# Four inner norms of a two-layer decoder trunk: roots by 32x32 turns on VectorE and a power on GpSimd instead of matmuls and an iteration

## The chip, the cores and the metric

The kernel runs on one core of one Trainium2 chip. The metric is device time in microseconds (us) of one execution; the value shown for a kernel is the median of its runs. A core has five engines that run beside each other, each in its own fixed order: TensorE (PE in the profile, with its weight loads as PEld), VectorE (DVE), ScalarE (ACT), GpSimd (POOL) and SyncE (SP, which here issues most DMAs). They wait for each other through semaphores. Matmuls accumulate in PSUM banks; everything else lies in SBUF.

## The reference, cut to what matters

The input is one sequence of 256 tokens of width 1024, in float32. There are two layers. Every norm is an RMS norm: each token is divided by the root of the mean of its squares (plus a small constant), and multiplied by a gain.

```python
def rms_norm(x, g):
    xf = x.astype(jnp.float32)
    y = xf * lax.rsqrt(jnp.mean(xf * xf, axis=-1, keepdims=True) + EPS)
    return (y * g.astype(jnp.float32)).astype(x.dtype)

# layer 0
x = x + short_conv_mixer(rms_norm(x, a_norm), a_w_in, a_conv, a_w_out)
x = x + conv_glu_ffn(rms_norm(x, f_norm[0]), f_w_up[0], f_conv[0], f_conv_b[0], f_w_down[0])
# layer 1
k_blk, v_blk, k_mean = shared_kv(x, kv_norm, w_k, w_v)
x = x + moba_attention(rms_norm(x, b_norm), w_q, w_o, k_blk, v_blk, k_mean, rel_bias)
x = x + conv_glu_ffn(rms_norm(x, f_norm[1]), f_w_up[1], f_conv[1], f_conv_b[1], f_w_down[1])
return rms_norm(x, final_norm)
```

`conv_glu_ffn` is an up projection to 2 x 2816, a causal convolution of width 3 along the tokens, silu(g) * v, and a down projection. The K/V norm and the norm of the attention see the same x, so they share one root per token and differ in their gains. That leaves four inner roots: mixer, feed-forward 0, shared K/V with queries, feed-forward 1. The final norm is computed in another way and is not touched.

## The kernel before

**Layout.** Activations stand transposed: `xT` is 128 partitions by 8 tiles by 256 tokens, so a token's features are spread over the partitions. Every float32 operand of a matmul is split into a high and a low part, and a product is three matmuls (`mm3`, lines 169 to 171: high x high, high x low part of x, low part of the weights x high).

**Weights.** They come in units: big ones ("B", 1 MB, in three raw buffers) and small ones ("S", 0.5 MB). For each unit a DMA fills `rawB` or `rawS`, ScalarE writes the high part (`hiB`, `hiS`, line 91) and VectorE the low part (`loB`, `loS`, line 97), which reads raw and high part. `hi("B")` and `lo("B")` take the next unit in order; `lo` then issues the DMA of the unit three later. The high and low buffers have two or three slots: `hi` of a unit waits until TensorE has finished the earlier unit in that slot. In the attention's part there are two slots, and the units come in the order v0, v1, v2, q0 to q7, v3 (v: values, q: queries and keys of two heads).

**Order.** Every engine's order is the order in which the program's lines issue instructions; there is no scheduler behind it. TensorE runs the units one after another without a break in the program: `up_step` for mixer and feed-forward, `v_step` and `qk_step` for the attention, 48 matmuls for each big unit.

**The roots.** The division by the root is put off: the matmuls take x times gain, and the roots are multiplied into the product as it leaves PSUM (`mixer_a` lines 456 and 465, `conv` line 551, `qk_out` line 678), or by columns for the values (`v_out`, lines 662 and 663). So the roots are wanted only when the first product is done. At each boundary `boundary()` adds the residual, writes the high and low parts of x (lines 283 and 287) and the squares (291), and adds the squares' tiles up to one row of 128 x 256 (296 to 299). Two helpers then make the roots:

- `rstd_cols` sums the 128 partitions by a matmul with a column of ones (line 342; its result stands as columns, token on partition), scales (346), takes the inverse root by a guess and three iterations on VectorE (327 to 332), and writes a diagonal matrix in a high and a low part (353, 354).
- `rstd_rows` multiplies a matrix of ones (`each`) with that diagonal (361), which gives every partition the whole row of roots, and ScalarE copies it to `rr` (364).

Some steps of TensorE's work are put between these two, so that the iteration has time; tile 0 of x is copied to a second address (`tile_0_again`, lines 278 and 279) for units that take tile 0 late. `bias_table` (lines 370 to 382) makes a table of the attention's bias on GpSimd at the program's start; it is stored to DRAM at line 630 and read in the attention.

In the attention's part `v_step(1)` carries the sums, `v_step(2)` the spreading; ScalarE's queue there holds the split of v2, then of q0, then `v_out(0)`, then the copy of the roots.

Of the kernel before, what the change touches and what calls it, by code (L numbers as in the profile page):

```python
# [13 lines left out]
I32 = mybir.dt.int32  # L14
# [28 lines left out]
def yoco_kernel(ctx: ExitStack, tc: tile.TileContext, t: dict, out: bass.AP):  # L43
# [95 lines left out]
    each = const.tile([128, 192], F32R, name="each")[:, 48:176]  # L139
# [5 lines left out]
    A.activation(each, ones, AF.Copy)  # L145
# [158 lines left out]
    def boundary(acc, x, gain, order=same, again=True):  # L304
# [20 lines left out]
    def rsqrt(ms, y, a, eng=V):  # L325

        eng.tensor_scalar(y.bitcast(I32), ms.bitcast(I32), -0.5, float(0x5F3759DF), op0=OP.mult, op1=OP.add)
        for _ in range(3):
            eng.tensor_mul(a, y, y)
            if eng is V:  # L330
                V.scalar_tensor_tensor(a, a, -0.5, ms, op0=OP.mult, op1=OP.mult)
                V.scalar_tensor_tensor(y, a, 1.5, y, op0=OP.add, op1=OP.mult)
            else:
                eng.tensor_mul(a, a, ms)
                eng.tensor_scalar(a, a, -0.5, 1.5, op0=OP.mult, op1=OP.add)
                eng.tensor_mul(y, a, y)

    def rstd_cols(sq, meanwhile=None):

        ps = psum.tile([128, 512], F32, name="misc", bufs=1)  # L340
        for c in range(2):
            PE.matmul(ps[:, c:c + 1], sq[:, 2, c * 128:(c + 1) * 128], ones[:, 0:1],
                      start=(c == 0), stop=True, skip_group_check=True)
        w = tmp.tile([128, 8], F32, name="nw")
        ms, y, a = w[:, 0:2], w[:, 2:4], w[:, 4:6]
        V.tensor_scalar(ms, ps[:, 0:2], 1.0 / D, EPS, op0=OP.mult, op1=OP.add)
        rsqrt(ms, y, a)
        if meanwhile:
            meanwhile()
        dh, dl = (tmp.tile([128, 384 + 64], F32R, name="d" + x, tag="z" + x, bufs=4)[:, 16:16 + S] for x in "hl")  # L350
        for c in range(2):
            d = slice(c * 128, c * 128 + 128)
            V.tensor_scalar(dh[:, d], ident, y[:, c:c + 1], None, op0=OP.mult)
            V.scalar_tensor_tensor(dl[:, d], ident, y[:, c:c + 1], f32(dh[:, d]), op0=OP.mult, op1=OP.subtract)
# [131 lines left out]
    for q in range(1, 4):  # L486
        quarter(q)
# [556 lines left out]
```

## Time and profile before

| | |
|---|---|
| Median of 3 runs | 568.18 us (567.7 to 568.34) |
| Profiled execution, its own time | 567.42 us |
| Its span, first to last instruction | 565.6 us |
| Mean granted TensorE clock | 0.997 |
| TensorE busy | 558.5 us, 99% of the span, 4908 matmul records |
| VectorE busy | 473.2 us, 84% |
| ScalarE busy | 341.7 us, 60% |
| GpSimd busy | 10.3 us, 2% |

How to read the rows quoted below: a row of the timeline has its start and its duration in us, the engine, the line in the kernel, the operation, output<-inputs with shapes, and xN where N like operations are merged (then the duration is from the first start to the last end). What stands in square brackets is idle time ahead of it, and what ended it. A row of a group has the count, then busy us, then the mean ns of one, then the idle time before. A float32 matmul that is not split by hand shows as several records (line 342: x4 for two). In the row of one tile's instructions, three numbers parted by strokes are the shortest, median and longest duration in ns.

### The profile page before, as it was taken

What the parts mean: (1) busy time and instruction counts of PE and PEld (TensorE: products, weight loads), DVE (VectorE), ACT (ScalarE), POOL (GpSimd) and SP (SyncE); (2) the same over time, 40 slices, a digit from 0 to 9 for tenths busy, and PEclk for the clock granted to TensorE, in tenths of its full rate; (3) what the DMA queues carried; (4) which work ended last, traced back from release to release, by engine and by line L of the source; (5) the groups of instructions that cost most, each with busy time, mean ns of one, the idle gap of its engine ahead of it and who ended that gap; (6) DMA issues with size and microseconds to landing.
All of it is one profiled execution on the core that took longest, in us unless ns stands there. A gap on an engine that the chain in (4) does not pass through costs nothing.

```text
span 565.6 us, 11827 instructions
## 1 busy us (share of the span) xinstructions
PE 558.5 (99%) x4908; PEld 554.9 (98%) x4908; DVE 473.2 (84%) x820; ACT 341.7 (60%) x526; POOL 10.3 (2%) x32
## 2 busy tenths in 40 slices
PE   9999999999999999999999999999999999999995
PEld 9999999999999999999999999999999999999995
DVE  6998869889877787778897999859999888889876
ACT  7765437566654565466757777556676456546534
POOL 0400000000000000000000000000000000000001
PEclk9999999999999999999999999999999999999998
DMA  8986573536546545655254556654656654563211
GB/s 304 387 298 218 203 282 112 175 134 259 190 178 224 202 164 194 224 189 184 90 211 163 203 207 213 194 177 150 224 187 224 224 195 163 203 222 118 71 38 75
DMA packets 24181, 108.48 MB, mean 192 GB/s; under 512 B 2736, under 2 KB 5440, under 8 KB 16192
## 3 DMA queue, kind: packets, MB, share of 16 engines
q1 hardware_dynamic: 23840, 107.43, 53.6%
q8 instruction: 38, 0.62, 0.4%
q10 hardware_dynamic: 288, 0.30, 0.2%
q14 instruction: 15, 0.12, 0.1%
HBM read 106.65 MB, written 1.07 MB: 190 GB/s over the span
## 4 chain that ended last, share of the span: by engine, by line
PE 98%; issue 0%; ACT 0%; DVE 0%; POOLq 0%; POOL 0%; ACTq 0%
PE up L169 20%; PE up L170 19%; PE up L171 19%; PE acc L169 7%; PE acc L170 7%; PE acc L171 7%; PE acc L202 3%; PE acc L203 3%; PE acc L200 3%; PE up L413 1%; PE up L783 1%; PE acc L653 1%; PE acc L656 1%; PE acc L655 1%; PE misc L142 1%; PE acc L708 1%
## 5 line engine op out<-in xcount | busy, mean ns | idle before, releaser
L169 PE MATMUL up<-xh,hiB 128*128 128x256 f32 x928 | 256.9, 277 | 0.0
L171 PE MATMUL up<-xh,loB 128*128 128x256 f32 x928 | 256.4, 276 | 0.0
L170 PE MATMUL up<-xl,hiB 128*128 128x256 f32 x928 | 256.3, 276 | 0.0
L169 PEld LDWEIGHTS up<-xh,hiB 128*128 128x128 f32 x928 | 174.2, 188 | 0.5 <-issue 0.3
L170 PEld LDWEIGHTS up<-xl,hiB 128*128 128x128 f32 x928 | 174.3, 188 | 0.0
L171 PEld LDWEIGHTS up<-xh,loB 128*128 128x128 f32 x928 | 174.2, 188 | 0.0
L97 DVE TENSOR_TENSOR loB<-rawB,hiB 128x2048 fp32r<-128x2048 f32 (+3 forms) x78 | 148.0, 1903 | 3.7 <-ACT hiB L91 3.6
L91 ACT ACTIVATE hiB<-rawB 128x2048 fp32r<-128x2048 f32 (+2 forms) x75 | 123.8, 1657 | 15.0 <-PE up L170 7.0
L558 ACT ACTIVATE cv<-u,pk 128x256 f32<-128x256 f32 x88 | 48.2, 595 | 69.3 <-DVE u L551 69.3
L97 DVE TENSOR_TENSOR loS<-rawS,hiS 128x1024 fp32r<-128x1024 f32 (+2 forms) x73 | 83.7, 1149 | 6.4 <-ACT hiS L91 6.0
L397 DVE SCALAR_TENSOR_TENSOR cv<-u,pk,cv 128x255 f32<-128x255 f32 x192 | 81.4, 481 | 2.7 <-ACT cv L558 1.7
L91 ACT ACTIVATE hiS<-rawS 128x1024 fp32r<-128x1024 f32 (+2 forms) x73 | 72.0, 988 | 8.9 <-PE acc L170 5.3
L551 DVE TENSOR_TENSOR u<-up,rr 128x512 f32<-128x512 f32 x44 | 30.3, 689 | 44.9 <-PE up L171 43.0
L171 PE MATMUL acc<-sh,loS 128*128 128x256 f32 x240 | 66.2, 276 | 0.0
L169 PE MATMUL acc<-sh,hiS 128*128 128x256 f32 x240 | 66.2, 276 | 0.0
L170 PE MATMUL acc<-sl,hiS 128*128 128x256 f32 x240 | 66.2, 276 | 0.0
L394 ACT ACTIVATE sh<-hid 128x256 fp32r<-128x256 f32 x52 | 21.7, 417 | 58.4 <-DVE hid L575 53.7
L171 PEld LDWEIGHTS acc<-sh,loS 128*128 128x128 f32 x240 | 45.1, 188 | 0.0
L170 PEld LDWEIGHTS acc<-sl,hiS 128*128 128x128 f32 x240 | 45.1, 188 | 0.0
L169 PEld LDWEIGHTS acc<-sh,hiS 128*128 128x128 f32 x240 | 45.0, 188 | 0.0
L200 PE MATMUL acc<-hiS,sh 128*128 128x256 f32 x154 | 42.5, 276 | 0.0
L202 PE MATMUL acc<-loS,sh 128*128 128x256 f32 x154 | 42.5, 276 | 0.0
(193 smaller groups left out, 795.5 us busy)
## 6 DMA issues: line engine op xcount, KB each, us to landing
rawB<-w_up SPq DMA_DIRECT2D x44, 1024.0 KB, 4.8
rawS<-w_dn SPq DMA_DIRECT2D x44, 512.0 KB, 3.4
rawB<-w_qk SPq DMA_DIRECT2D x8, 1024.0 KB, 4.9
rawB<-w_mc SPq DMA_DIRECT2D x6, 1024.0 KB, 7.6
rawS<-w_mo SPq DMA_DIRECT2D x8, 512.0 KB, 4.9
rawB<-w_v SPq DMA_DIRECT2D x4, 1024.0 KB, 4.7
rawS<-w_o SPq DMA_DIRECT2D x8, 512.0 KB, 4.1
rawS<-w_mb SPq DMA_DIRECT2D x7, 512.0 KB, 5.2
```

Source lines behind the costliest of these rows:

```text
L91: A.activation(self.hi[:, c], self.raw[:, c], AF.Copy)
L97: V.tensor_sub(self.lo[:, c], self.raw[:, c], f32(self.hi[:, c]))
L169: PE.matmul(o, wh, xh, start=start, stop=False, skip_group_check=True)
L170: PE.matmul(o, wh, xl, start=False, stop=False, skip_group_check=True)
L171: PE.matmul(o, wl, xh, start=False, stop=stop, skip_group_check=True)
L200: PE.matmul(o, hh[:, tok], u.hi[:, f], start=(first and (apart or d.start == 0)), stop=False, skip_group_check=True)
L202: PE.matmul(o, hh[:, tok], u.lo[:, f], start=False, stop=False, skip_group_check=True)
L203: PE.matmul(o, hl[:, tok], u.hi[:, f], start=False, stop=last, skip_group_check=True)
L394: return (h, lw), lambda: A.activation(h, src, AF.Copy), lambda: V.tensor_sub(lw, src, f32(h))
L397: V.scalar_tensor_tensor(o[:, back:], u[:, :S - back], w, o[:, back:], op0=OP.mult, op1=OP.add)
L551: V.tensor_mul(u, ub[j], rr[:, 0:1, :].to_broadcast([128, 2, S]))
L558: A.activation(o[:, half, :], u[:, half, :], AF.Identity, scale=cw[half][2], bias=par(P_FCB, c0 + half * FJ))
```

## The change

`rstd_cols`, `rsqrt` and `rstd_rows` go, with the matrix `each`. In their place:

- `roots` turns the 128 x 256 row of partial sums by 32x32 blocks on VectorE (line 326 of the new kernel), so that in each group of 32 partitions a token stands on a partition, reduces each block to one number (327; 128 x 8), brings the four groups of partitions to the first 32 with three copies (329), adds them (331) and scales (332). GpSimd raises the 32 x 8 numbers to the power -0.5 (333). After some other work of VectorE (`meanwhile`) three copies (337) give all four groups of partitions the roots.
- `rows` turns them back with each root repeated 32 times (342), which fills `rr` on all partitions.
- For the values, four copies (831) put the roots as columns into `ycol`.

Around them: `boundary` takes the low part of the weights in one piece and no longer copies tile 0 again; the second address is used in fewer units; TensorE's units are no longer cut in two around the sums; `bias_table` is issued behind the first `roots`.

```diff
@@ start @@
-    each = const.tile([128, 192], F32R, name="each")[:, 48:176]
+    sums = const.tile([128, 64], F32, name="sums")
+    ycol = const.tile([128, 64], F32, name="ycol")
+    halves = const.tile([128, 64], F32, name="halves")
+    G.memset(halves, -0.5)
...
-    A.activation(each, ones, AF.Copy)
@@ boundary @@
         sum_squares(sq, 0)
-        lo("B", 0, 2)
-        if not again:
-            lo("B", 1, 2)
+        lo("B")
         sum_squares(sq, 1, order)
-        if again:
-            lo("B", 1, 2)
-            tile_0_again(xh, xl)
         return xh, xl, sq
@@ the helpers @@
-    def rstd_cols(sq, meanwhile=None):
...
+    def roots(sq, meanwhile=None):
+
+        y = tmp.tile([128, 8], F32, name="nw")
+        t = sq[:, 3, :]
+        V.transpose(t, sq[:, 2, :])
+        V.tensor_reduce(sums[:, 0:8], t.rearrange("p (b i) -> p b i", i=32), axis=mybir.AxisListType.X, op=OP.add)
+        for a in range(1, 4):
+            V.tensor_copy(sums[0:32, 8 * a:8 * a + 8], sums[32 * a:32 * a + 32, 0:8])
+        ms = sums[0:32, 32:40]
+        V.tensor_reduce(ms, sums[0:32, 0:32].rearrange("p (a b) -> p b a", a=4), axis=mybir.AxisListType.X, op=OP.add)
+        V.tensor_scalar(ms, ms, 1.0 / D, EPS, op0=OP.mult, op1=OP.add)
+        G.tensor_tensor(y[0:32, :], ms, halves[0:32, 0:8], op=OP.pow)
         if meanwhile:
             meanwhile()
...
+        for a in range(1, 4):
+            V.tensor_copy(y[32 * a:32 * a + 32, :], y[0:32, :])
+        return y
+
+    def rows(y, r):
+
+        V.transpose(r, y.rearrange("p (b o) -> p b o", o=1).to_broadcast([128, 8, 32]))
@@ mixer @@
-    ext = bias_table()
...
-    _, dg = rstd_cols(sq, lambda: quarter(0))
-    for q in range(1, 4):
+    y = roots(sq, lambda: (quarter(0), quarter(1)))
+    ext = bias_table()
+    rr = root_rows()
+    rows(y, rr[:, 0, :])
+    for q in range(2, 4):
         quarter(q)
@@ feed-forward, unit 1 @@
-                _, dg = rstd_cols(sq)
-                lo("S")
+                rr = root_rows()
+                y = roots(sq, lambda: lo("S"))
+                rows(y, rr[:, 0, :])
                 A.activation(first, ones[:, 0:1], AF.Silu)
...
-                rr = rstd_rows(dg)
                 gate(0, conv(0))
@@ attention, after v_step(1) @@
-                ycol, dg = rstd_cols(sq)
...
+                y = roots(sq, lambda: scaled_lo(xT, P_BN, range(0, 4), xqh, xql))
                 oh = Heads("oh")
+                rr = root_rows()
+                rows(y, rr[:, 1, :])
+                A.activation(rr[:, 0, :], rev(rr[:, 1, :]), AF.Copy, scale=-0.125)
             elif n == 2:
-                v_step(2, range(0, 3))
-                rr = rstd_rows(dg, (-0.125, 1.0), (rev, same))
-                v_step(2, range(3, 8))
+                v_step(2)
...
             elif n == 1:
-                scaled_lo(xT, P_BN, range(0, 4), xqh, xql)
                 hi("B")
                 lo("B")
                 tile_0_again(xvh, xvl)
                 tile_0_again(xqh, xql)
                 scaled_lo(xT, P_BN, range(4, 8), xqh, xql)
+                for a in range(4):
+                    d = slice(32 * a, 32 * a + 32)
+                    V.tensor_copy(ycol[d, 0:2], y[d, a::4])
                 v_out(0)
```

Two places in the order of instructions show what the lists of lines don't. Both are in the attention's part, while TensorE works on v1 and v2. In ScalarE's order, the numbered hiB are high parts: before, 3694 is v2, 3779 is q0 and 3854 is q1; after, 3668 is v2, 3747 is q0 and 3820 is q1. Before:

```order
L91 ACTIVATE hiB_3694<-rawB 128x2048
L854 ACTIVATE vh<-xh 128x256
L283 ACTIVATE xh<-xres,pk 128x256 x2
L91 ACTIVATE hiB_3779<-rawB 128x2048
L278 ACTIVATE xh<-xh 128x256 x2
L662 ACTIVATE vs<-acc,nw 128x256
L364 ACTIVATE rr<-misc 128x256 x2
L91 ACTIVATE hiB_3854<-rawB 128x2048
L662 ACTIVATE vs<-acc,nw 128x256 x2
L871 ACT_TABLE_LOAD
```

ScalarE at the same place with the change:

```order
L91 ACTIVATE hiB_3668<-rawB 128x2048
L819 ACTIVATE vh<-xh 128x256
L285 ACTIVATE xh<-xres,pk 128x256 x2
L809 ACTIVATE rr<-rr 128x256
L91 ACTIVATE hiB_3747<-rawB 128x2048
L280 ACTIVATE xh<-xh 128x256 x2
L627 ACTIVATE vs<-acc,ycol 128x256
L91 ACTIVATE hiB_3820<-rawB 128x2048
L627 ACTIVATE vs<-acc,ycol 128x256 x2
L838 ACT_TABLE_LOAD
```

The roots' step on ScalarE moved from behind q0's high part and v_out(0) to ahead of q0's high part, and it now reads what VectorE's turn writes, no longer a PSUM bank; v_out(0) reads `ycol`.

VectorE's order at this place, where loB are the low parts of the same units (before, 3781 is q0 and 3856 is q1; after, 3749 is q0). Before, from the last step of the diagonal on:

```order
L354 SCALAR_TENSOR_TENSOR dl<-ident,nw,dh 128x128
L287 SCALAR_TENSOR_TENSOR xl<-xres,pk,xh 128x256 x4
L97 TENSOR_TENSOR loB_3781<-rawB,hiB_3779 128x2048
L279 CAST xl<-xl 128x256 x2
L287 SCALAR_TENSOR_TENSOR xl<-xres,pk,xh 128x256 x4
L663 TENSOR_SCALAR vs<-acc,nw 128x256
L97 TENSOR_TENSOR loB_3856<-rawB,hiB_3854 128x2048
```

VectorE with the change, from the first turn on:

```order
L326 STREAM_TRANSPOSE sq<-sq 128x256
L327 TENSOR_REDUCE sums<-sq 128x8
L329 COPY sums<-sums 32x8 x3
L331 TENSOR_REDUCE sums<-sums 32x8
L332 TENSOR_SCALAR sums<-sums 32x8
L289 SCALAR_TENSOR_TENSOR xl<-xres,pk,xh 128x256 x4
L337 COPY nw<-nw 32x8 x3
L342 STREAM_TRANSPOSE rr<-nw 128x256
L97 TENSOR_TENSOR loB_3749<-rawB,hiB_3747 128x2048
L281 CAST xl<-xl 128x256 x2
L289 SCALAR_TENSOR_TENSOR xl<-xres,pk,xh 128x256 x4
L831 COPY ycol<-nw 32x2 x4
```

The four steps on xl stand where they stood, but they are now inside the roots' chain, between the scaled sums and the copies; the second turn stands ahead of q0's low part, and the copies to `ycol` behind the second four steps, ahead of v_out(0) and of q1's low part.

More of the change, by code (lines that the diff above doesn't have):

```diff
@@ L302, in square_tile, with boundary @@
         return act.tile([128, KT, S], F32, name="sq", tag="oh", bufs=1)
-    def boundary(acc, x, gain, order=same, again=True):
+    def boundary(acc, x, gain, order=same):
         xh, xl = parts_tiles()
@@ L338, in rstd_cols @@
-    def rstd_cols(sq, meanwhile=None):
[L340 to L347, printed above, removed]
+    def roots(sq, meanwhile=None):
[9 more added lines that the diff above has]
+        G.tensor_tensor(y[0:32, :], ms, halves[0:32, 0:8], op=OP.pow)
@@ L348, in rstd_cols @@
         if meanwhile:
             meanwhile()
[L350 to L354, printed above, removed]
-        return y, (dh, dl)
-    def rstd_rows(dg, scales=(1.0,), orders=(same,)):
-        ps = psum.tile([128, 512], F32, name="misc", bufs=1)
-        for n in range(2):
-            PE.matmul(ps[:, :S], each, dg[n], start=(n == 0), stop=(n == 1), skip_group_check=True)
-        r = act.tile([128, 2, S], F32, name="rr", bufs=1)
-        for n, s in enumerate(scales):
-            A.activation(r[:, n, :], orders[n](ps[:, :S]), AF.Copy, scale=s)
-        return r
+        for a in range(1, 4):
+            V.tensor_copy(y[32 * a:32 * a + 32, :], y[0:32, :])
@@ L477, in yoco_kernel @@
     mc[1] = acc_bank()
-    up_step(MC[1], mc[1], xh, xl, 2, range(1, 8), first=1)
-    MC[1].used = False
+    up_step(MC[1], mc[1], xh, xl, 2, (*range(1, 7), 0, 7), first=1, again=True)
     def quarter(q):
@@ L489, in yoco_kernel @@
     hi("B")
-    up_step(MC[1], mc[1], xh, xl, 2, (0,), first=1, again=True)
-    MC[1].used = True
     mb[1] = acc_bank()
-    up_step(MB[1], mb[1], xh, xl, 1, (*range(1, 7), 0, 7), first=1)
+    up_step(MB[1], mb[1], xh, xl, 1)
     mc[2] = up_bank()
-    up_step(MC[2], mc[2], xh, xl, 2, range(0, 2))
-    rr = rstd_rows(dg)
     A.activation(rr[:, 1, :], rr[:, 0, :], AF.Square)
     lo("S")
-    up_step(MC[2], mc[2], xh, xl, 2, range(2, 8))
+    up_step(MC[2], mc[2], xh, xl, 2)
     mb[2] = psum.tile([128, 512], F32, name="misc", bufs=1).rearrange("p (a s) -> p a s", s=S)
@@ L507, in yoco_kernel @@
     mc[3] = up_bank()
-    up_step(MC[3], mc[3], xh, xl, 2, (1, 2, 3, 4, 5, 6, 0, 7), first=1, again=True)
+    up_step(MC[3], mc[3], xh, xl, 2)
     mixer_b(2, mixer_a(2, "S"))
@@ L631, in yoco_kernel @@
     acc = ffn(0, xh, xl, sq)
-    xvh, xvl, sq = boundary(acc, xT, P_KVN, rev, again=False)
+    xvh, xvl, sq = boundary(acc, xT, P_KVN, rev)
     xqh, xql = parts_tiles()
@@ L641, in yoco_kernel @@
     vb, qb, qs, sb, pr, pt, ps_, ob, bias = {}, {}, {}, {}, {}, {}, {}, {}, {}
-    ycol = rr = None
+    rr = None
     def v_step(n, ks=range(KT), first=0, again=False):
```

36 lines of the change are left out of this document (6 added, 30 removed).

## The prediction

> **What bounds the kernel now.** I read the table of busy time first, then the shares of the chain that ended last, then TensorE's rows one by one.
>
> ```profile
> PE 558.5 (99%) x4908; PEld 554.9 (98%) x4908; DVE 473.2 (84%) x820; ACT 341.7 (60%) x526; POOL 10.3 (2%) x32
> PE 98%; issue 0%; ACT 0%; DVE 0%; POOLq 0%; POOL 0%; ACTq 0%
> 17.65 0.28 PE L171 MATMUL acc<-xh,loB 128*128 128x256 f32 x1
> 18.67 0.28 PE L171 MATMUL acc<-xh,loB 128*128 128x256 f32 x1
> ```
>
> TensorE is the chain: 98% of it, with no engine ahead of it anywhere after the first microseconds. Nine matmuls lie between the two L171 rows, so one costs 1.02 / 9 = 0.113 us, and this step repeats through the program. Two things follow. A matmul taken out is a full gain, and a wait put ahead of TensorE is a full loss; what happens on the other engines counts only where it makes TensorE wait.
>
> **What is removed on TensorE.** Per norm: two sums by a column of ones (L342, each two records) and two products that spread the roots (L361).
>
> ```profile
> 18.78 0.50 PE L342 MATMUL misc<-ones,sq 128*128 128x1 f32 x4
> 19.14 0.37 PE L169 MATMUL acc<-xh,hiB 128*128 128x256 f32 x1
> 19.34 0.28 PE L170 MATMUL acc<-xl,hiB 128*128 128x256 f32 x1
> L342 PE MATMUL misc<-ones,sq 128*128 128x1 f32 x16 | 2.0, 229 | 0.0
> L361 PE MATMUL misc<-dl,each 128*128 128x256 f32 x4 | 1.1, 278 | 0.0
> ```
>
> From L342's start to the second matmul behind it are 0.56 us, of which one ordinary step remains: 0.45 saved. L361 saves two steps, 0.23. So 0.68 per norm and 2.7 us for the four, if nothing new is waited for.
>
> **What is added.** VectorE now does per norm a turn and a reduction of 128x256, three small copies, a second small reduction and a scaling; GpSimd a power of 32x8; VectorE three copies and a second turn. The prices:
>
> ```profile
> L756 DVE STREAM_TRANSPOSE late<-pr 32x128 f32<-32x128 f32 x40 | 12.2, 304 | 0.7
> L937 DVE STREAM_TRANSPOSE xt<-xres 32x512 f32<-32x512 f32 x16 | 11.2, 702 | 0.5
> L299 DVE TENSOR_TENSOR sq<-sq 128x256 f32<-128x256 f32 x4 | 1.7, 427 | 0.1
> 284.30 0.16 DVE L329 TENSOR_TENSOR nw<-nw 128x2 f32<-128x2 f32 x1
> 284.50 0.16 DVE L331 SCALAR_TENSOR_TENSOR nw<-nw 128x2 f32<-128x2 f32 x1
> 557.50 0.57 POOL L962 TENSOR_TENSOR nl<-nl 128x1 f32<-128x1 f32 x1
> 559.12 0.22 POOL L976 TENSOR_SCALAR nl<-nl 128x1 f32<-128x1 f32 x1 [1.04 <-ACT junk L953]
> ```
>
> A turn of 256 columns lies between 128 and 512: 0.44 us. No row shows a reduction; I take the add of 128x256, 0.43 (between 0.24, half of the two casts of L279 at 291.03 below, and 0.69, the 128x512 at 21.54). Small dependent steps follow each other every 0.20 us (if independent copies overlap, 0.10). So the scaled sums stand 0.44 + 0.43 + 5 x 0.20 = 1.87 us after the start. The power is known for one column: 0.57 us. Eight columns cost from 0.57 (side by side) to 0.22 + 8 x 0.35 = 3.0 (one after another, 0.35 being power less plain operation); I take 1.3, nearer to the measured row.
>
> **Where the new chain is hidden.** In the two feed-forward blocks it is.
>
> ```profile
> 99.75 1.22 DVE L97 TENSOR_TENSOR loB<-rawB,hiB 128x1024 fp32r<-128x1024 f32 x1
> 104.42 1.22 DVE L97 TENSOR_TENSOR loS<-rawS,hiS 128x1024 fp32r<-128x1024 f32 x1
> 106.67 0.69 DVE L551 TENSOR_TENSOR u<-up,rr 128x512 f32<-128x512 f32 x1 [1.04 <-ACT rr L364]
> 110.86 0.28 PE L169 MATMUL up<-xh,hiB 128*128 128x256 f32 x1
> ```
>
> The weights' loB and the sums of squares are through near 101.0 us, as before (99.75 + 1.22; only their order changes). 1.87 for the sums, 1.22 of loS meanwhile, then the power, 0.6 for copies and 0.44 for the turn give 106.4; L551, the first product with the roots, started at 106.67. TensorE needs its bank only at 110.86 (0.7 earlier now). Nothing is lost. Layer 1 has the same order.
>
> In the mixer it just fits.
>
> ```profile
> 19.47 0.15 DVE L346 TENSOR_SCALAR nw<-misc 128x2 f32<-128x2 f32 x1
> 21.54 0.69 DVE L97 TENSOR_TENSOR loB<-rawB,hiB 128x512 fp32r<-128x512 f32 x1
> 22.66 0.28 PE L169 MATMUL up<-xh,hiB 128*128 128x256 f32 x1
> 101.80 0.33 SPq L630 DMA_DIRECT2D ext_d<-ext  x1
> 277.15 2.36 DVE L97 TENSOR_TENSOR loB<-rawB,hiB 128x1024 fp32r<-128x1024 f32 x2
> ```
>
> From 19.47 the sums end at 21.35 and quarter 0 of the weights at 22.0; TensorE, 0.45 earlier, reads it at 22.66 - 0.45 + 0.23 = 22.44. The power starts when quarter 0 is through (below), ends at 23.35; copies, turn and quarter 2 end at 25.1, and TensorE wants quarter 2 at 22.2 + 24 x 0.113 + 0.23 = 25.15. I count 0. bias_table, moved behind this power on GpSimd, took 6 us (20.7 to 26.4, rows below) and is stored only at 101.80: 75 us of cover, nothing if it moves by 3. `each` and the copies of tile 0 were on ScalarE and VectorE beside a busy TensorE: 0. lo("B") in boundary() is now one piece everywhere; ahead of K/V two halves took 2.36 us and one takes 2.29 (row below), so it is no later.
>
> **Where it is not hidden: shared K/V.** ScalarE's copy of the roots (now L809) stands ahead of the split of q0's weights (hiB, L91) in ScalarE's queue, and v_out(0) behind it now waits for four more copies on VectorE. Before:
>
> ```profile
> 281.70 2.29 DVE L97 TENSOR_TENSOR loB<-rawB,hiB 128x2048 fp32r<-128x2048 f32 x1 [0.20 <-ACT hiB L91]
> 285.81 1.92 ACT L91 ACTIVATE hiB<-rawB 128x2048 fp32r<-128x2048 f32 x1 [3.04 <-PE acc L656]
> 287.24 1.67 DVE L287 SCALAR_TENSOR_TENSOR xl<-xres,pk,xh 128x256 fp32r<-128x256 f32 x4
> 288.25 0.46 ACT L662 ACTIVATE vs<-acc,nw 128x256 f32<-128x256 f32 x1
> 288.60 0.65 ACT L364 ACTIVATE rr<-misc 128x256 f32<-128x256 f32 x2
> 288.82 2.29 DVE L97 TENSOR_TENSOR loB<-rawB,hiB 128x2048 fp32r<-128x2048 f32 x1
> 291.03 0.49 DVE L279 CAST xl<-xl 128x256 fp32r<-128x256 f32 x2
> 291.56 1.92 ACT L91 ACTIVATE hiB<-rawB 128x2048 fp32r<-128x2048 f32 x1 [2.31 <-issue]
> 293.01 0.48 DVE L663 TENSOR_SCALAR vs<-acc,nw 128x256 f32<-128x256 f32 x1
> 294.22 1.28 ACT L871 ACT_TABLE_LOAD   x1
> 291.31 0.28 PE L169 MATMUL up<-xh,hiB 128*128 128x256 f32 x1
> 296.86 0.28 PE L169 MATMUL up<-xh,hiB 128*128 128x256 f32 x1
> ```
>
> q0's loB ended at 291.1 and TensorE came to q0 at 291.31: 0.2 us of slack. Now, on the same clock:
> - VectorE is free at 283.9; sums end 285.8; four L287 (1.6) end 287.4; the power starts behind the first of them (286.2) and ends 287.5; copies 288.1; turn 288.55.
> - L809, 0.33 us, ends 288.9; hiB of q0, 1.92, ends 290.8; its loB, 2.29, ends 293.1.
> - TensorE, 0.68 earlier, wants that loB with its third matmul at 290.85. **First stall: 2.25 us.**
> - Behind loB (start 290.8) VectorE does the casts and four L287 as before, 293.01 - 288.82 = 4.2, and four copies of ycol, 0.8: 295.8. v_out(0) on ScalarE, 0.35, then q1's hiB, which used to start at 291.56 and waits behind it: 298.05; its loB: 300.35.
> - TensorE runs q0 from 293.1 and wants q1's loB 5.55 us later (291.31 to 296.86), at 298.65. **Second stall: 1.7 us.**
>
> q2 is back in step: its hiB follows two v_out (0.8) and the table load (1.28, and 0.2 behind it), near 300.4, its loB ends near 304.6, and TensorE reaches q2 near 305.8.
>
> The sum: -2.7 + 2.25 + 1.7 = **+1.25 us**. Against the profiled execution, 567.42 us (span 565.6 and 1.8 around it), that is 568.7; it lies 0.76 below the median shown, so the median becomes 568.18 + 1.25 = **569.4**.
>
> **A rule weighed.** GpSimd and VectorE get in each other's way in this trace.
>
> ```profile
> L380 POOL TENSOR_SCALAR ext<-rb x16: 215/249/1178, 20.7 to 26.4; 16x3 f32<-16x3 f32 x3, 16x4 f32<-16x4 f32 x2, 16x6 f32<-16x6 f32 x2, 16x10 f32<-16x10 f32 x2
> 23.33 1.89 DVE L97 TENSOR_TENSOR loB<-rawB,hiB 128x512 fp32r<-128x512 f32 x3
> 25.13 1.22 DVE L97 TENSOR_TENSOR loS<-rawS,hiS 128x1024 fp32r<-128x1024 f32 x1
> ```
>
> GpSimd's small operations take 249 ns in the median and 1178 at most, about the length of the two-input L97 beside them; the three L97 keep their 0.60 us step. So I let the power wait for the VectorE operation in progress and VectorE not wait for it. The Trainium skill, "SBUF — State Buffer", section "Who interferes with whom", says more: a GpSimd operation that reads SBUF and a VectorE operation with two SBUF inputs exclude each other, and whichever starts first holds the port for its whole duration. By its first half the trace agrees; by its second half VectorE would stand during the power, which no row here shows. It is a rival below, priced from rows.
>
> **Rivals.**
> - *The stalls are hidden* (other side). If the whole chain took 2.4 us instead of 4.65, rows() ending by 286.3, q0's hiB would end early enough: 2.7 us faster, 565.5. For it: little; the 1.58 us of L287 alone lie in the chain.
> - *Cheap chain.* Independent copies at 0.10, reduction at 0.24, power hidden under L287: stalls of 1.5 and 1.3, net +0.1, up to +1.1 with mixed prices; about 568.8. For it: the power's measured 0.57.
> - *VectorE stands during the power.* Three L287 wait to 287.5 and end 288.7 instead of 287.4: +1.2 at q0; in the mixer quarter 1 waits and quarter 2 comes 0.6 late. +3.05: 571.2.
> - *Columns of the power one after another*, 3.0 us: +1.7 at q0 and +1.65 in the mixer: 572.8. For it: 0.35 us more than a plain operation for one column.
> - *The matmuls' removal saves nothing* would need TensorE to wait in their place; no row of idle time is there.
>
> **How the numbers follow.** Chances: forecast 0.52 (own range +0.9 to +2.0), cheap 0.24, VectorE standing 0.10, serial power 0.08, hidden 0.06. A measurement of this kernel can tell about 0.2%, 1.14 us, from no change: the forecast lies above that with 0.37 and below with 0.15. Slower: 0.37 + 0.10 + 0.08 = 0.55; same: 0.15 + 0.24 = 0.39; faster 0.06. The range leaves out the hidden case and the serial power, 0.14: 568.0 to 571.3.
>
> **What would show it.** After: no L342 or L361 rows; TensorE idle before q0's and q1's third matmul, released by VectorE's loB, about 2 us each; ScalarE idle ahead of L809, released by the turn; GpSimd's row of 32x8 near 1.3 us. If L809 starts before 286.5 or q0's hiB starts ahead of it, I am wrong and it is faster; a power above 2 us, or gaps among the L287 rows, makes it slower than said.

## The result, and the profile after

| | before | after |
|---|---|---|
| Median | 568.21 us (10 executions, 567.68 to 568.44) | 571.48 us (10 executions, 571.16 to 580.77) |
| Profiled execution, its span | 567.42 us, 565.6 | 571.21 us, 569.4 |
| Mean granted TensorE clock | 0.997 | 0.994 |
| Ratio after to before | | 1.008, 95% interval 1.0059 to 1.0102 |

The change makes the kernel slower by 3.0 us and a little more in six of ten executions (571.16 to 571.66 us). The other four took 576.40, 576.44, 580.26 and 580.77 us, at granted clocks of 0.995 to 0.998 where the six had 0.994 to 0.996; in 77 executions of all the comparisons here the kernel before stays at 567.42 to 569.09 us but for one of 625.13 us, at a granted clock of 0.85. The ratios leave out executions over 1.5% above a kernel's fastest (here the two of 580 us), and since for this change the long ones turn out to belong to the program, I give the executions' times beside them. So there are two things to explain: 3 us in every execution, and 5 to 10 us more in some.

The page of the kernel after, the table of busy time and the shares of the chain:

```profile
PE 559.4 (98%) x4884; PEld 554.4 (97%) x4884; DVE 472.2 (83%) x803; ACT 339.3 (60%) x519; POOL 20.9 (4%) x37
PE 87%; DVE 5%; ACT 3%; issue 2%; DMA 1%; POOL 1%; SPq 0%; POOLq 0%; ACTq 0%; DVEq 0%
```

The 24 matmul records of L342 and L361 are gone, and yet TensorE is busy for longer (558.5 us before), and 13% of the chain is now on other engines (2% before). TensorE's timeline in K/V, at the place of the first stall foretold:

```profile
291.23 0.28 PE L172 MATMUL up<-xl,hiB 128*128 128x256 f32 x1
293.33 0.57 PE L173 MATMUL up<-xh,loB 128*128 128x256 f32 x1 [1.82 <-DVE loB L97]
293.70 0.41 PE L171 MATMUL up<-xh,hiB 128*128 128x256 f32 x1
```

From 291.23 to 293.33 us are 2.10, of which one step of 0.12 is ordinary: 2.0 us lost to q0's loB. ScalarE's timeline says why:

```profile
288.73 0.42 ACT L809 ACTIVATE rr<-rr 128x256 f32<-128x256 f32 x1 [5.94 <-DVE rr L342]
289.05 1.90 ACT L91 ACTIVATE hiB<-rawB 128x2048 fp32r<-128x2048 f32 x1
```

ScalarE stood 5.94 us ahead of L809 for VectorE's second turn, with q0's hiB behind it in the queue. But the steps from 293.70 us on are nearly twice as long (0.21 us). The view by windows (length, then busy time and count of TensorE, weight loads, VectorE, ScalarE and GpSimd, then the granted clock, the DMA share and GB/s):

```profile
293.40:296.80 3.40, 3.40 (x16) 3.40 (x17) 2.82 (x11) 0.91 (x2) 0.00 (x0) 0.50 0.68 234
296.80:300.00 3.20, 3.20 (x29) 3.20 (x29) 1.88 (x2) 3.18 (x4) 0.00 (x0) 1.00 0.66 243
```

For 3.4 us the granted clock is 0.50; 16 matmuls run where 30 would have, 1.6 us lost. The second stall that I had foretold, at q1, is not there: TensorE came to q1 late enough.

GpSimd's timeline has the four powers:

```profile
22.28 2.05 POOL L333 TENSOR_TENSOR nw<-sums,halves 32x8 f32<-32x8 f32 x1 [20.77 <-DVE sums L332]
103.85 2.59 POOL L333 TENSOR_TENSOR nw<-sums,halves 32x8 f32<-32x8 f32 x1 [71.12 <-DVE sums L332]
285.93 1.74 POOL L333 TENSOR_TENSOR nw<-sums,halves 32x8 f32<-32x8 f32 x1 [19.32 <-DVE sums L332]
392.69 2.49 POOL L333 TENSOR_TENSOR nw<-sums,halves 32x8 f32<-32x8 f32 x1 [105.02 <-DVE sums L332]
```

They take 1.74 to 2.59 us, not 1.3, and VectorE waits 0.94, 1.56, 0.35 and 1.52 us behind them (the last wait ends with a fill of 0.09 us that GpSimd does right behind the power). Small gaps of TensorE follow where I had counted none, the largest in the second feed-forward:

```profile
39.87 0.28 PE L172 MATMUL acc<-sl,hiS 128*128 128x256 f32 x1
40.16 0.39 PE L173 MATMUL acc<-sh,loS 128*128 128x256 f32 x1
415.58 0.28 PE L172 MATMUL up<-xl,hiB 128*128 128x256 f32 x1
416.16 0.39 PE L173 MATMUL up<-xh,loB 128*128 128x256 f32 x1 [0.30 <-DVE loB L97]
```

By the distance of such rows, less 0.113, there are about 0.8 us of them in the mixer (18.95, 39.87, 51.06) and 0.9 us in the second feed-forward (398.95, 415.58), with about 0.11 us in each for the step behind the wait.

Part by part, by TensorE's rows in the two profiled executions (before, then after): from MC[1]'s first matmul to the first feed-forward 79.63 and 79.73 us, the first feed-forward 180.45 and 179.52, from v0 to the attention's first scores 28.97 and 32.53, the second feed-forward 179.3 and 179.3. So only the first feed-forward keeps what the removed matmuls save; the gaps use it up in the mixer and in the second, and K/V loses 3.6 us net. (Of the 3.8 us between the two spans, 0.85 lie ahead of MC[1], which started at 14.0 to 14.9 us in the traces of all the kernels here.)

### The profile page after: what moved, and what is told of

It is laid out like the page before. It is cut to its first block, busy times and chain, and to the rows that moved or that the text cites. A ratio compares the mean times of both kernels' runs of the same rounds, so it can differ in the third digit from the quotient of the medians.

```text
span 569.4 us, 11768 instructions
## 1 busy us (share of the span) xinstructions
PE 559.4 (98%) x4884; PEld 554.4 (97%) x4884; DVE 472.2 (83%) x803; ACT 339.3 (60%) x519; POOL 20.9 (4%) x37
## 4 chain that ended last, share of the span: by engine, by line
PE 87%; DVE 5%; ACT 3%; issue 2%; DMA 1%; POOL 1%; SPq 0%; POOLq 0%; ACTq 0%; DVEq 0%
PE up L173 18%; PE up L171 18%; PE up L172 18%; PE acc L173 6%; PE acc L171 6%; PE acc L172 6%; PE acc L204 3%; PE acc L205 3%; PE acc L202 3%; DVE loB L97 2%; ACT hiB L91 2%; PE up L748 1%; DMA xres<-xT 1%; PE acc L673 1%; POOL nw L333 1%
## 5 line engine op out<-in xcount | busy, mean ns | idle before, releaser
L97 DVE TENSOR_TENSOR loB<-rawB,hiB 128x2048 fp32r<-128x2048 f32 (+2 forms) x75 | 147.5, 1971 | 6.8 <-ACT hiB L91 6.7
```

The source lines that it names most:

```text
L97: V.tensor_sub(self.lo[:, c], self.raw[:, c], f32(self.hi[:, c]))
```

## The experiments

Four theories stood or grew: **1**, K/V's order (L809 ahead of q0's hiB, v_out(0) ahead of q1's) and the clock that drops behind the stall; **2**, the long power makes VectorE late; **3**, the removed matmuls give 2.7 us; and **4**, found in the first four runs, TensorE's own step. The times below are of single executions unless a ratio is given; the kernel before had medians of 568.08 to 568.36 us on the same chips.

### K/V's order, and the power

```diff
                 rows(y, rr[:, 1, :])
-                A.activation(rr[:, 0, :], rev(rr[:, 1, :]), AF.Copy, scale=-0.125)
...
             elif n == 1:
                 hi("B")
+                A.activation(rr[:, 0, :], rev(rr[:, 1, :]), AF.Copy, scale=-0.125)
                 lo("B")
...
-                v_out(0)
             elif n == 2:
                 hi("B")
                 lo("B")
+                v_out(0)
                 v_out(1)
```

The first line moved alone, the second alone, and both:

> The changed kernel with one line moved: the ScalarE copy of L809 stands behind q0's hi("B") instead of ahead of it. Theory 1 (the loss is K/V's order): q0's loB ends some 2.2 us earlier, at about the time TensorE wants it, so the 2.0 us idle before the third matmul of q0 goes, and with it the 3.4 us of granted clock 0.50 that follow it (1.6 us): 571.4 - 3.6 = 567.8 us if nothing else is late, 569.5 us if q1's hiB, behind v_out(0), now shows the 1.7 us stall that the halved clock had covered. Theory 2 (the loss is the long power, spread over four norms, and the halved clock has nothing to do with the idle time): at most 2.0 us go, 569.4 us, and the clock is still 0.50 after 293 us.

> The changed kernel with only v_out(0) moved behind q1's hi("B") and lo("B"). Theory 1: the first stall and the halved clock are ahead of it and stay, and q1's loB was not late in the changed kernel, so the time stays at 571.4 us within 0.3. Theory 2: the same. A rival in which v_out(0) is what keeps TensorE slow (its ScalarE copy runs from 295.9 us) would give 569.7 us and full clock from 293 us.

> Both moves. Theory 1: no stall at q0, full clock there, no stall at q1: 571.4 - 3.6 = 567.8 us, and under the kernel before by some 0.4 us. If the run with L809 alone is slower than this one by about 1.7 us, the second stall is real once the first is gone; if they agree, q1's loB has room. Theory 2: 569.4 us at best.

In the fourth, `op=OP.pow` became `op=OP.mult`:

> The changed kernel with GpSimd's power replaced by a multiplication of the same 32x8 tile: the inner norms' roots are left out. Theory 2: the 1.7 to 2.6 us of each power fall to about 0.2 us; VectorE no longer waits 0.9 us in the mixer and 1.5 us in the second feed-forward, and the TensorE gaps behind it (0.6 us in the mixer, 0.9 us in the second feed-forward) go; K/V's chain ends 1.5 us earlier, so its 2.0 us stall shrinks to about 0.5 us and the clock stays full: 571.4 - 1.5 - 1.5 - 1.6 = 566.8 us. Theory 1 (the copy of L809 and not the power decides K/V; the power's waits elsewhere are covered): L809 still stands ahead of q0's hiB and comes 1.5 us earlier, so 571.4 - 1.5 - 1.6 = 568.3 us, with the small gaps of the mixer and the second feed-forward unchanged.

Measured: 568.62, 577.60, 578.68, 584.50 us with L809 moved; 569.59 to 586.06 us in seven executions with v_out(0) moved (ratio 1.0034, 1.0015 to 1.0052); 575.93 to 583.22 us with both (1.0182, 1.0108 to 1.0256); 568.89 to 569.82 us in nine executions without the root and one of 580.18 (1.0021, 1.0011 to 1.0031). But for 568.62 us, between the two numbers of the first expectation, and 569.59 us, near the rival's number in the second, the times of the first three missed on the wrong side; those of the fourth lie above both of its numbers (566.8 and 568.3). The traces of the first three said what theory 1 had said. With L809 moved there is no stall at q0 and no halved clock, and the second stall stands where I had put it (TensorE's timeline):

```profile
305.90 0.28 PE L172 MATMUL up<-xl,hiB 128*128 128x256 f32 x1
307.41 0.39 PE L173 MATMUL up<-xh,loB 128*128 128x256 f32 x1 [1.23 <-DVE loB L97]
```

That is 1.4 us. With v_out(0) moved alone the first stall and the halved clock stay; with both, neither stall is there and the clock is never 0.50 between the warm-up and the end. So theory 1 holds for K/V, and the time goes somewhere else.

Without the root GpSimd's four rows show what the power is:

```profile
21.83 0.58 POOL L333 TENSOR_TENSOR nw<-sums,halves 32x8 f32<-32x8 f32 x1 [20.31 <-DVE sums L332]
102.94 1.12 POOL L333 TENSOR_TENSOR nw<-sums,halves 32x8 f32<-32x8 f32 x1 [71.80 <-DVE sums L332]
285.03 0.30 POOL L333 TENSOR_TENSOR nw<-sums,halves 32x8 f32<-32x8 f32 x1 [19.33 <-DVE sums L332]
391.46 1.06 POOL L333 TENSOR_TENSOR nw<-sums,halves 32x8 f32<-32x8 f32 x1 [106.13 <-DVE sums L332]
```

Row for row the power takes 1.43 to 1.47 us more than a multiplication. The rest, 0.3 to 1.1 us, follows the length of the two-input operation that VectorE has just begun (loS of 1.23 us in the feed-forwards, 0.65 us in the mixer, 0.42 us in K/V), as it did in the trace of before. VectorE itself does not stand: loS takes 1.23 us beside the power and beside the multiplication. The gaps of the second feed-forward are gone in this run, and that of 39.87 us: theory 2 is right about them. In K/V the chain got only 0.35 us shorter, since the four L289 (1.65 us) lie beside the power there, the stall was still 1.9 us and the clock halved behind it; my expectation of 0.5 us had forgotten that cover.

### TensorE's step

Where did 10 us go in the version with both moves? TensorE was busy, at full clock, without waits. Its windows, first of that version, then of the kernel before:

```profile
150.00:250.00 100.00, 100.00 (x851) 100.00 (x851) 73.51 (x106) 54.08 (x71) 0.00 (x0) 1.00 0.51 187
430.00:530.00 100.00, 100.00 (x885) 100.00 (x884) 88.26 (x128) 59.74 (x78) 0.00 (x0) 1.00 0.55 201
```

```profile
150.00:250.00 100.00, 100.00 (x885) 100.00 (x884) 77.43 (x110) 57.50 (x75) 0.00 (x0) 1.00 0.53 190
430.00:530.00 100.00, 100.00 (x884) 100.00 (x884) 86.96 (x126) 57.71 (x75) 0.00 (x0) 1.00 0.50 180
```

The same matmuls run 851 or 885 to 100 us: a step of 117.5 or 113.0 ns (with the ends, 117.8 and 113.3), both perfectly regular, and nothing lies between them. In the version with both moves the slow step begins at 39.9 us, behind a gap like that of 39.87 above, and ends at 323 us in the attention: 284 us at 4.5 ns in 118, 11 us. This gap was there in the profile of the change too, and the fast step followed it. In the kernel before, the slow step comes behind L342 (100.45 and 386.42 us) and lasts 3 to 4 us. Theory 4 was then: the removed matmuls break the row and re-set the step. The next runs put matmuls back whose result nothing reads, at the old places, into the version with both moves:

```diff
+    def odd_sums():
+
+        ps = psum.tile([128, 512], F32, name="misc", bufs=1)
+        for c in range(2):
+            PE.matmul(ps[:, c:c + 1], ones, ones[:, 0:1], start=(c == 0), stop=True, skip_group_check=True)
+
+    def odd_rows(u, xh, xl):
+
+        ps = psum.tile([128, 512], F32, name="misc", bufs=1)
+        for n in range(2):
+            PE.matmul(ps[:, :S], u.hi[:, :128], (xh, xl)[n][:, 1, :], start=(n == 0), stop=(n == 1), skip_group_check=True)
```

> The version with both moves in K/V, and at the places of the kernel before, in the mixer, both feed-forwards and K/V, matmuls whose result nothing reads: two of 128x1 (as the old sums of squares) and two of 128x256 (as the old rows). Theory 4 (TensorE's step is 113.3 or 117.8 ns and stays what it is until something breaks the row of matmuls; the old norms' matmuls were such breaks): the version with both moves spent 39 to 323 us in the slow step and took 576.9 us; here a slow step lasts some microseconds, so the executions lie within about 1 us of each other at 566.8 + 4 x 0.68 = 569.5 us, none above 572 us. Rival (the long executions have nothing to do with the program's matmuls, the chip is in another condition): they stay among 575 to 586 us in at least a third of the executions. Theory 3 (the removed matmuls were worth 0.68 us for each norm) takes its size from this run against the version with both moves where that runs at the fast step.

> The same with the two 128x256 matmuls alone at each norm. They are of the same shape as their neighbours and should not break the row. Theory 4 in its narrow form (a break needs another shape or a wait): executions above 574 us stay, the fast ones are at 566.8 + 4 x 0.23 = 567.7 us. If all executions are at 567.7 us, a change of bank alone is enough to end a slow step.

> The same with the 128x1 matmuls alone. Theory 4: they are the breaks. After them either step may follow (in the kernel before it was the slow one in two of three cases), so executions may differ by up to 5 us, from 566.8 + 4 x 0.45 = 568.6 us to about 573 us, but none should hold the slow step from the mixer to K/V unchanged past a norm's matmuls. The rival says as many executions of 575 to 586 us as without them.

A fourth run widened the work beside the power (MC[1] also takes tile 0 last, as before):

```diff
-    y = roots(sq, lambda: (quarter(0), quarter(1)))
+    y = roots(sq, lambda: (quarter(0), quarter(1), quarter(2)))
...
-                y = roots(sq, lambda: lo("S"))
+                y = roots(sq, lambda: (lo("S"), lo("B", 0, 2)))
...
-            if not last:
-                lo("B")
+            if not last:
+                lo("B", j == 0, 1 + (j == 0))
```

> The version with both moves, and more of VectorE's work beside the powers: three quarters of the second weight's lo part in the mixer in place of two, half of the next lo part in the feed-forwards beside loS; MC[1] takes tile 0 last. Theory 2 (the power's 2 to 2.6 us make VectorE late, and about 1 us of TensorE's gaps in the mixer and the second feed-forward come of it): the gaps at 18.8, 39.7 and 405 us go, 566.8 - 1.0 = 565.8 us where the step is fast. Theory 4 adds: with fewer breaks a slow step taken at the start lasts to K/V, so some executions are above 574 us.

Measured: with both kinds 584.70 to 585.13 us, with the 128x1 matmuls alone 583.84 to 584.88 us (1.0284, 1.027 to 1.0297), four executions each, all of them long. With the 128x256 matmuls 567.38 us once and 572.87 to 574.16 us seven times. Theory 4 as I had put it was wrong, in the most useful way: the 128x1 matmul does not cure the slow step, it causes it: in both traces the slow step stands behind the first of them, at 20.5 us, and stays to K/V, and stands again behind that of the second feed-forward. (With the 128x1 matmuls alone TensorE had been slow from 5 us too, but ran the last three matmuls ahead of that first one at the fast step again.) The run with 128x256 matmuls alone (1.0075, 1.0051 to 1.01) shows the price of one half of the program, by windows:

```profile
150.00:250.00 100.00, 100.00 (x885) 100.00 (x884) 77.44 (x110) 57.50 (x75) 0.00 (x0) 1.00 0.53 190
430.00:530.00 100.00, 100.00 (x851) 100.00 (x851) 82.65 (x121) 54.29 (x73) 0.00 (x0) 1.00 0.50 180
```

Fast in the first feed-forward, slow in the second from 395 us to the end: 573.0 - 567.4 = 5.6 us. The version with the wider cover ran at 566.44 to 566.83 us four times, and at 572.11 to 585.06 us eight times (1.0017, 0.9987 to 1.0046). In its trace the waits of the mixer are nearly gone (0.2 us are left), but not that of the second feed-forward, which is 0.8 us at 410.67 us.

So what ends the slow step in the kernel before? It ends at 104.5 us, while TensorE runs the 25th to 30th matmul behind L342, and those are the six of tile 0, which step 1 of a feed-forward took next to last and from its second address (`again=True`). The change had removed those reads as well, in MC[3], in steps 1, 2 and 6 of the feed-forwards, in v1 and at q0. Put back in MC[3] and steps 2 and 6:

```diff
+            if i in (2, 6):
+                up_step(up[i], ub[i], xh, xl, 2, (*range(1, 7), 0, 7), first=1, again=True)
+            else:
                 up_step(up[i], ub[i], xh, xl, 2)
...
-    up_step(MC[3], mc[3], xh, xl, 2)
+    up_step(MC[3], mc[3], xh, xl, 2, (1, 2, 3, 4, 5, 6, 0, 7), first=1, again=True)
...
-                y = roots(sq, lambda: lo("S"))
+                y = roots(sq, lambda: (lo("S"), tile_0_again(xh, xl)))
```

> The version with both moves in K/V, and the reads of tile 0's second copy put back in MC[3] and in steps 2 and 6 of each feed-forward (the change had taken them out with the matmuls). Theory 4, as the last runs mend it: a 128x1 matmul, and now and then a wait, puts TensorE on the step of 117.8 ns, and what puts it back to 113.3 ns is the step that reads the second copy from another address. Then a slow step taken in the mixer ends at step 2 of the first feed-forward at the latest, some 68 us or 2.6 us of time: executions at 566.8 us, some to 569.4 us, none above 571 us. Rival (the second copies do nothing, the slow step ends by chance): executions of 573 to 585 us as before, in half of the cases or more.

> The same put back into the version with more of VectorE's work beside the powers, which ran at 566.5 us and, in 8 of 12 executions, at 572 to 585 us. Theory 4: 566.5 us in most, none above 570 us; faster than the kernel before by 0.3%. Rival: the spread stays.

The kernel before with these reads taken out is the sharpest of the runs, since theory 4 says 581 us and everything else says 568:

```diff
-    up_step(MC[3], mc[3], xh, xl, 2, (1, 2, 3, 4, 5, 6, 0, 7), first=1, again=True)
+    up_step(MC[3], mc[3], xh, xl, 2)
...
-                up_step(up[1], ub[1], xh, xl, 2, (*range(n, 7), 0, 7), first=1, again=True)
+                up_step(up[1], ub[1], xh, xl, 2, range(n, 8))
...
-                up_step(up[i], ub[i], xh, xl, 2, ks, first=int(again), again=again)
+                up_step(up[i], ub[i], xh, xl, 2, range(n + 1 if i == 2 else 0, 8))
```

> The kernel before, with its norms' matmuls, where MC[3] and the feed-forwards read tile 0 in its place and in order, like the changed kernel. Theory 4: the 128x1 matmuls at 100 and 386 us put TensorE on the slow step in every execution, and nothing ends it until K/V and the end: about 175 and 170 us at 4 ns in 114, 6.5 + 6.3 us, so 568.2 + 12.8 = 581 us in every execution. Rival (chance, or the chip): 568.2 us within 0.5, perhaps with a few long executions.

Measured: 580.71, 580.75, 581.12 and 581.44 us (1.0228, 1.0214 to 1.0241). Its windows:

```profile
60.00:100.00 40.00, 40.00 (x355) 40.00 (x355) 32.55 (x49) 21.23 (x30) 0.00 (x0) 1.00 0.58 207
150.00:250.00 100.00, 100.00 (x851) 100.00 (x850) 74.78 (x107) 54.93 (x71) 0.00 (x0) 1.00 0.51 183
430.00:530.00 100.00, 100.00 (x852) 100.00 (x851) 84.03 (x121) 55.88 (x74) 0.00 (x0) 1.00 0.53 193
```

Fast up to the L342 of the first feed-forward, slow behind it. With the reads put back the version with both moves ran at 566.95 to 567.93 us in eight of eleven executions (569.94, 570.83 and 577.53 the others; ratio 1.000, 0.9986 to 1.0014), and the version with the wider cover at 566.18 to 566.74 us in five of seven (568.89 and 576.08; 0.998, 0.9967 to 0.9993). In the trace of the latter one sees it at work, in windows behind a gap of the second feed-forward and around step 6 (424 us):

```profile
412.00:423.50 11.50, 11.50 (x100) 11.50 (x99) 11.35 (x19) 8.71 (x12) 0.00 (x0) 1.00 0.64 229
425.00:436.00 11.00, 11.00 (x100) 11.00 (x99) 10.56 (x16) 6.61 (x10) 0.00 (x0) 1.00 0.66 256
```

100 matmuls in 11.5 us, then in 11.0. Three further runs asked whether the reads alone cure the change, whether address or order does it, and what the few long executions are. In the second, `again=True` is taken out of the kernel before and the order kept; in the third, `i in (2, 6)` becomes `i % 4 == 2`:

> The changed kernel with the reads of tile 0's second copy put back in MC[3] and in steps 2 and 6 of the feed-forwards, and nothing else: K/V keeps its order. Theory 1 and 4 together: the K/V loss (2.0 us of idle time and 1.6 us of halved clock) stays, the long executions of the changed kernel (576.4 to 580.8 us in four of ten) go: 571.2 us within 0.7 in nearly all. If the second copies were also what the K/V loss hung on, it would be near 567.5 us.

> The kernel before, with the order of the tiles as it was (0 next to last in MC[3] and in steps 1, 2 and 6 of the feed-forwards), but tile 0 read in its place and not from the second copy. If the other address ends the slow step, nothing ends it here: 581 us as where order and address were both plain (580.7 to 581.4). If the order ends it: 568.2 us.

> The version with more beside the powers and the second copy read in steps 2 and 6, which ran at 566.2 to 566.7 us and in two of seven executions at 568.9 and 576.1 us: here the second copy is read in every fourth step from 2 on. If those two were slow steps taken inside a feed-forward, behind step 6, they last at most four steps (1 us): 566.2 to 567.7 us in all. If executions of 575 us and more stay, they are something that the second copies don't end.

Measured: 580.90 to 581.29 us with the order alone (1.0229, 1.0216 to 1.0242), so it is the other address (in that order; the address alone was not run). The change with the reads put back took 570.49 to 571.38 us in five of six executions, and 573.75 once (1.006, 1.0043 to 1.0076): no execution of 576 us or more among six where there were four in ten, but 2.7 us of the 3 stay. With the reads in every fourth step eight of nine lie within 566.27 to 567.10 us and one at 575.55 (0.9977, 0.9967 to 0.9986). So three of 27 executions of these versions, at 575 to 578 us, are not ended by it. None of them was profiled. Two traces of other versions have a lead. In the version with L809 alone moved, TensorE was slow from 7 us and passed MC[1]'s read of the second address, at 19.1 to 19.7 us, without leaving the slow step:

```profile
8.80:18.80 10.00, 10.00 (x87) 10.00 (x87) 9.32 (x20) 8.76 (x18) 0.00 (x0) 1.00 1.03 391
20.00:35.00 15.00, 15.00 (x129) 15.00 (x129) 13.59 (x28) 8.99 (x12) 10.45 (x19) 1.00 0.92 347
150.00:250.00 100.00, 100.00 (x852) 100.00 (x851) 73.51 (x105) 53.81 (x70) 0.00 (x0) 1.00 0.52 188
```

That version had no later read before K/V. The run of the next section had them all, and in its trace TensorE, slow from 8 us, passed four in a row without leaving the slow step: MC[1]'s, MC[3]'s (36.1 us), that of step 2 (112.4 us) and that of step 6 (144.6 us). The first three lie ahead of its first artificial wait. Behind MC[3]'s, behind step 2's and behind step 6's:

```profile
37.00:111.00 74.00, 74.00 (x630) 74.00 (x630) 60.64 (x96) 37.77 (x50) 2.59 (x1) 1.00 0.56 201
114.00:127.00 13.00, 13.00 (x113) 13.00 (x112) 11.64 (x20) 7.46 (x14) 0.00 (x0) 1.00 0.52 191
146.00:154.00 8.00, 8.00 (x70) 8.00 (x70) 6.27 (x9) 4.61 (x6) 0.00 (x0) 1.00 0.47 175
```

(At the fast step these would be some 655, 117 and 73 matmuls.) So several reads in a row can fail, and the size fits the three long executions: from 8 us to v1, some 270 us at 4.5 ns in 118 are 10 us, and they lie 9 to 10 us above the others. What tells these slow steps from those that a read ended, at nine places in the mixer and the feed-forwards of seven traces, stays open; two of the nine had begun by 8 us too.

K/V has a slow step of its own. In each of the nine traces that reach v1 at the fast step, v1's first matmul begins the slow one, with neither a wait nor a 128x1 matmul ahead. (Its moving operand, the weights, lies 128 bytes into its buffer, and v0's at the start of its own; whether this does it, no run shows.) In the kernel before, v1's read of the second copy ends it 4.7 us later and q0's ends another; no run put these two back, and in the version with the reads in every fourth step it lasts to the scores:

```profile
278.40:301.40 23.00, 23.00 (x198) 23.00 (x197) 19.50 (x38) 12.82 (x16) 1.74 (x1) 1.00 0.62 212
```

The fast step has some 205 there. From v0 to the scores this version takes 28.86 us and the kernel before 28.97, though 0.68 us of matmuls are gone: some 0.6 us are still lost.

### The clock behind a wait

```diff
+            if layer == 0 and i in GAPS:
+                ps = psum.tile([128, 512], F32, name="misc", bufs=1)
+                for n in range(2):
+                    PE.matmul(ps[:, n:n + 1], ones, sq[:, 0, 0:1], start=(n == 0), stop=True, skip_group_check=True)
+                    if n == 0:
+                        G.memset(sq[:, 0:GAPS[i], :], 0.0)
```

These lines went into the version with both moves and the reads put back:

> The first of these kernels with six waits of TensorE for GpSimd put into the first feed-forward, behind steps 4, 7, 10, 13, 16 and 19: between two matmuls of 128x1 GpSimd fills 1, 2, 4, 5, 6 and 8 tiles of 128x256 with zeros (what was there is used no more). By the 0.53 us of the 128x512 fill of before the waits are some 0.6, 0.9, 1.4, 1.6, 1.9 and 2.4 us long. Theory 1's second half (TensorE's idle time halves its clock): the waits to 1.5 us leave the clock at 1.00, those from 2.0 us up are followed by 3.4 us at 0.50. Rival (the halved clock in K/V comes from something else there): the clock is 1.00 behind all six.

Measured, at 587.91 and 590.05 us: idle times of 0.50, 0.70, 1.15, 1.34, 1.55 and 2.01 us by TensorE's rows, of which these are the last three rows; then the windows around the fourth, and those behind the fifth and the sixth:

```profile
208.92 0.38 PE L575 MATMUL misc<-sq,ones 128*128 128x1 f32 x2 [1.34 <-POOL sq L577]
236.52 0.38 PE L575 MATMUL misc<-sq,ones 128*128 128x1 f32 x2 [1.55 <-POOL sq L577]
265.28 0.55 PE L575 MATMUL misc<-sq,ones 128*128 128x1 f32 x2 [2.01 <-POOL sq L577]
```

```profile
207.00:211.00 4.00, 2.66 (x23) 2.57 (x23) 3.50 (x4) 2.77 (x3) 1.17 (x1) 1.00 0.18 75
238.05:241.46 3.41, 3.41 (x19) 3.41 (x18) 3.11 (x7) 2.02 (x4) 0.00 (x0) 0.50 0.69 223
265.35:268.77 3.42, 3.42 (x16) 3.42 (x17) 3.42 (x6) 2.76 (x3) 0.00 (x0) 0.50 0.42 96
```

The first four leave the clock alone, the last two halve it for 3.4 us: the rival falls. The fifth wait ended at 236.52, and the clock dropped only at 238.05 us, 1.5 us later; the two drops are 27.30 us apart, eight times 3.41. The Trainium skill, "TensorE: Matmul & The Clock Gate", in Part 1 on the clock gate, says that activity is judged in windows of about 3.4 us that run on by themselves; the two drops agree. If so, whether a wait near this length costs the clock would depend on where in a window it falls; no run moved a wait to test that, but the change with the reads put back shows the other outcome in K/V:

```profile
292.79 0.38 PE L173 MATMUL up<-xh,loB 128*128 128x256 f32 x1 [1.82 <-DVE loB L97]
300.00 0.38 PE L173 MATMUL up<-xh,loB 128*128 128x256 f32 x1 [1.30 <-DVE loB L97]
```

```profile
292.50:296.00 3.50, 3.21 (x27) 3.21 (x28) 2.92 (x12) 0.66 (x2) 0.00 (x0) 1.00 0.66 204
```

The same idle 1.82 us, the clock at 1.00 behind it, and the second stall, 1.5 us, in its place.

## Why the prediction was wrong

It said 569.4 us and named 568.0 to 571.3; the six shorter executions lie at 571.2 to 571.7 and the median of all ten at 571.48. Two steps failed, both terms put at nothing: "nothing is lost" and "just fits" for the roots' lateness outside K/V (measured 0.9 and 0.8 us, 0.4 of the latter for a copy of tile 0), and 0 for tile 0's copies (5 to 9 us in four executions of ten). That 571.2 is also the price of the rival in which VectorE stands, and so the upper end of the range, is chance: that rival fell.

- **Where K/V loses: right.** L809 ahead of q0's hiB gave a first stall of 2.0 us (2.25 said) and v_out(0) ahead of q1's a second of 1.5 us (1.7 said), the latter in the runs in which the clock held. In the profiled execution 1.6 us of halved clock stand in its place. Either way some 3.6 us where 3.95 were said. That the halved clock costs about what the second stall would have is luck: the forecast had no clock in it. Moving the two lines back brings the change with the second address from 570.8 to 567.75 us in the median.
- **The chain: right; the power's 1.3 us: too short.** The added operations cost what was said (turn 0.44, reduction 0.42, small steps about 0.2). The power is 1.45 us above a multiplication, whose shortest row is 0.30, and what VectorE's operation adds comes on top. A power above 2 us was named as a sign of a slower kernel, and three of the four are. The rival in which VectorE stands fell.
- **"Nothing is lost" in the feed-forwards and "just fits" in the mixer: wrong.** I had asked whether the roots would be there when wanted, and in the first feed-forward they were. But VectorE waits up to 1.6 us for them, and the low parts of the next weights stand behind that wait on an engine that is 83% busy. Their lateness reaches TensorE some 20 us later, at 415.58. Why the same wait of VectorE (1.56 us) leaves no gap in the first, no run here shows. With the powers gone, these gaps went, but for that at 18.95; with more work beside them the kernel took 0.9 us less, though not in the second feed-forward. Together with tile 0's copy, which the new order in MC[1] wants earlier (18.95 us), this is about 1.7 us that the sum counted as 0, nearly all of the 1.8 us by which 571.2 exceeds the forecast.
- **The removed matmuls, 2.7 us: right where it can be isolated.** The version with both moves and that with both kinds of matmuls put back run at the slow step through the whole first feed-forward, in 186.56 us (96.35 to 282.91) and 187.25 us (97.17 to 284.42): 0.69 for this norm, 0.68 said. The other three are not isolated; the best versions are 1.3 to 1.5 us under the kernel before, with 0.77 us of waiting at 410.6 us and some 0.6 us of slow step in K/V, which is about 2.7 in all.
- **"The copies of tile 0 were on ScalarE and VectorE beside a busy TensorE: 0."** This is the step that cost most where it struck. I priced the copies and not what they did: reads from the second address end TensorE's slow step in most places. Without them a slow step taken at some wait in the mixer lasts into the attention, one taken in the second feed-forward to the end. The run with 128x256 matmuls puts 5.6 us on the latter; the four long executions are 5.2 and 9.3 us above the six others. None of the four was itself profiled, so their sorting into the two places is argued. That the reads remove most of the spread is shown by the runs with and without them (executions of 575 us or more: four in ten and none in six, four in four and one in eleven, five in twelve and one in seven); that they always do is not so.

**The version that runs below both in eight of nine executions** is the change with L809 and v_out(0) moved behind q0's and q1's splits, more of VectorE's work beside the powers, and the second address in every fourth step: 566.27 to 567.10 us, 0.2% under the kernel before (0.9977, 0.9967 to 0.9986). The ninth, at 575.55 us, is the reason not to call it finished.

## What to carry to other kernels

An operation whose result is wanted late can still be early in a queue: when a chain gets a longer way round, ask what is queued behind each of its waiting instructions, on ScalarE (hiB behind L809) and on VectorE (the low parts behind the power), and look for the damage later too (here up to some 20 us). Before removing code that seems to be worth nothing (a second copy, an odd order), take it out alone and measure: here that alone was worth 13 us in the kernel before. And a time that spreads, where the kernel before did not, is a finding about the program until a run says otherwise.

## What the runs showed of the hardware

- A row of equal matmuls (128x128 weights, 256 columns) runs at one of two steps, 113.3 or 117.8 ns, at full granted clock, and keeps it for long (the slow one for 306 us in the trace with L809 alone moved). A 128x1 matmul put it on the slow one at each of the eight places in the feed-forwards of five traces where TensorE arrived at the fast one (between the artificial waits the fast one followed once), v1's first matmul did so in nine traces of nine, a wait now and then. In the mixer and the feed-forwards, reads of the moving operand from another address put it back at nine places in seven traces, and did not at five places in two traces; q2's, in the attention, did not in four. Why the address does it, and why it sometimes does not, no run here shows.
- Idle times of TensorE from 1.55 us up were followed by 3.4 us at half clock, at 1.82 us in one run and not in another; none to 1.34 us was.
- GpSimd's power of 32x8 takes 1.45 us more than its multiplication, and the rows of both grow with VectorE's two-input operation beside them (the multiplication 0.30 us beside 0.42, 0.58 beside 0.65, 1.06 and 1.12 beside 1.23).
